# DeltaNet output gated by z where it is turned, q and k norms on VectorE, and no two-tensor work on GpSimd in the attention of a hybrid encoder step

## The chip, the core and the metric

The kernel runs on one core of one Trainium2 chip. The metric is the device time of one execution in microseconds (us). The core's engines have queues of their own, each worked off in order: TensorE (PE) multiplies and transposes, VectorE (DVE), ScalarE (ACT) and GpSimd (POOL) work on elements, and SyncE (SP) issues most of the DMAs. An instruction waits at the head of its queue until the semaphores that it names have been raised.

## What is computed

One layer of an encoder for 592 tokens of width 1024 (16 meta tokens and 512 of a prompt, and 64 of a sample stream with 256 cached keys). All of it is in float32.

```python
h = _rmsnorm(x, p["norm1"])
qa, ka, va, qkv_b, z_b, beta_b, alpha_b, gate_a, gate_b = jnp.split(h @ p["w_in"], SPLITS, axis=-1)
# branch A: differential attention, 8 heads, two 64-wide maps each
qa = _rmsnorm(qa.reshape(bsz, t, A_HEADS, 2, A_HEAD_DIM), p["q_norm"])
ka = _rmsnorm(ka.reshape(bsz, t, A_HEADS, 2, A_HEAD_DIM), p["k_norm"])     # also an output
o_a = attend(qa, ka, va, lam)
o_a = (_rmsnorm(o_a, p["sub_norm"]) * (1.0 - lam_init)).reshape(bsz, t, A_V_WIDTH)
# branch B: gated DeltaNet, 8 heads of 128
o_b, s_new = _gated_delta(qb, kb, vb, g, beta, ssm0.astype(f32))
z = jax.nn.silu(z_b.astype(f32)).reshape(bsz, t, B_HEADS, B_HEAD_DIM)
o_b = (_rmsnorm(o_b, p["gdn_norm"]) * z).reshape(bsz, t, B_WIDTH).astype(x.dtype)
# merge and channel mixer
mix = jax.nn.sigmoid(gate_a + p["b_gate"][0]) * (o_a @ p["w_br_a"]) + jax.nn.sigmoid(gate_b + p["b_gate"][1]) * (o_b @ p["w_br_b"])
x = x + mix @ p["w_out"]
h2 = _rmsnorm(x, p["norm2"])
x = x + jnp.square(jax.nn.relu(h2 @ p["w_up"])) @ p["w_down"]
```

## The kernel before

**Products in two parts.** Every large product is made of three: an operand x is kept as a high part in a reduced float32 format and the low part x minus high (names ending in h and l), and high x high, low x high and high x low are summed in PSUM. Weights come from DRAM in pieces of 128x1024 (wr), ScalarE casts the high part (wh), and the low part (wl) is subtracted by VectorE or GpSimd. `VG(out, n)` chooses between these two by the planned clocks of the engines.

**The stream of tasks and the chains.** `tasks` lists the large products in order: DeltaNet's q, k, v (pg_d), the gate z (pg_z), the attention's q, k, v for pairs of heads p (pg_a, the task names a, p and 0, 1 or 2), the merge gates B between them and A after them (pg_g), branch B (pg_bb), branch A (pg_ba), out (pg_o), up and down (pg_u, pa_dn to pd_dn). Beside them run chains, Python generators: the DeltaNet of four heads (`delta(0)`, `delta(1)`), for each head of the attention its preparation (`attend_prep`), 40 units of scores (`unit`, five for each head), the end of a head (`finish`), and `load_ob`. A planner (`Pace`) keeps a clock for each engine with fixed costs for instructions and transfers. `drive` writes some matmuls of the stream, then lets each chain whose last results are due by the planned clock of TensorE write its next stage. The order on every engine's queue comes out of this, before the kernel runs; it is not changed on the chip.

**Around the change.** `z_tasks` make z times (1 + tanh) of it, halved elsewhere, and store it in z_d. At the end of `delta(g)` the output of a tile of tokens (vtok) is scaled by its norm (c1), TensorE turns it (pf), ScalarE scales it by gdn_norm into oT, and SP stores it in ob_d. `load_ob` loads ob_d and z_d (tiles ma and mb), GpSimd multiplies them, and when the last task of gate A has read the hidden state (hh, hl), their high and low parts are written over it, for branch B. `attn_tasks` evict the projections (st) by a copy on ScalarE and store them in at_d; their squares give the norms' factors (rn). `attend_prep` loads q, k and v of a head, GpSimd multiplies q and k by rn and k by its weight (kn_bc), and k goes out as a result. Then TensorE turns k and q (ptk, ptq) and they are split (akT, aqT). A unit makes the scores (psc); VectorE adds the bias and takes the extremum (the ISA rows, `soft`), ScalarE exponentiates; VectorE joins the two maps (`combine`: mx<-mx,lam, then sc<-sc,mx); TensorE turns the weights (pwT), they are copied (wT), and it multiplies by v (ppo). `finish` makes a head's norm (aorv, aort, aory), scales (osb), turns (pot) and stores it in oa_d. The first three tasks of branch B may run beside the attention; the attention over, `load_oa` brings oa_d through two buffers (oa) and splits it (oh, ol) for branch A. Branch B's gate comes through tiles thb, its result goes to mb_d.

Of the kernel before, what the change touches and what calls it, by code (L numbers as in the profile page):

```python
# [17 lines left out]
P = 128  # L18
# [192 lines left out]
def stream_step_kernel(  # L211
# [74 lines left out]

    def VG(out, n):

        if "tail" in done:
            return V  # L290
        return V if max(pace.t["DVE"], pace.t["PE"]) + 1.05 * n <= max(pace.t["POOL"], pace.t["PE"]) + out * n else G

# [293 lines left out]
    th_d = [[dp.tile([P, TQ], F32, name=f"th_d{i}{j}") for j in range(KC)] for i in range(2)]  # L586
    qkv_d = [[dp.tile([P, 640 if i == 2 else T], F32, name=f"qkv_d{i}{j}") for j in range(4)] for i in range(3)]
    at_d = [dp.tile([H, P, NT, P], F32, name=f"at_d{i}") for i in range(3)]
    z_d, oa_d, mb_d = ([dp.tile([P, TQ], F32, name=f"{nm}{j}") for j in range(KC)] for nm in ("z_d", "oa_d", "mb_d"))
    ob_d = dp.tile([H, P, T], F32, name="ob_d")  # L590
    m_d = [dp.tile([4, 20, 32, 32], F32, name=f"m_d{i}") for i in range(2)]
    yi_d = [dp.tile([80, 1024], F32, name=f"yi_d{i}") for i in range(2)]
# [288 lines left out]
    def delta(g):  # L881
# [250 lines left out]
        r = rsqrt(db, c2, 20, 1.0 / P, EPS, tag="or")  # L1132
        V.scalar_tensor_tensor(c1, c1, 0.5, r, ALU.mult, ALU.mult)
        yield
        for s in range(NT + 1):
            if s:
                c0, n = TILES[s - 1]
                pf = bank(f"pf{g}{s}").rearrange("p (h i) -> p h i", h=4)
                for h in range(4):
                    TE.transpose(pf[:, h, :n], vtok[s - 1][:n, h], ident[:n, :n])  # L1140
                oT = a2(f"oT{s}")
                S.activation(oT[:, :, :n], pf[:, :, :n], AF.Copy, scale=gdn_col)
                store(ob_d[h0:h0 + 4, :, c0:c0 + n].rearrange("h d i -> d h i"), oT[:, :, :n])
            if s < NT:
                n = TILES[s][1]
                V.tensor_tensor(vtok[s][:n], vtok[s][:n], c1[:n, 4 * s:4 * s + 4, None].to_broadcast([n, 4, P]), ALU.mult)
            yield
# [31 lines left out]
    def z_tasks(cs):  # L1179
        out = []  # L1180
        for c in cs:
            def evac(h, ps, a, b, c=c):
                j = 2 * c + h
                if a == 0:
                    finish_convs(0)
                    gts["z"] = gp.tile([P, TQ], F32, name=f"zt{j}", tag="gth")
                th = gts["z"]
                S.activation(th[:, a:b], ps, AF.Tanh, scale=0.5)
                V.scalar_tensor_tensor(th[:, a:b], th[:, a:b], 1.0, ps, ALU.add, ALU.mult)
                if b == TQ:  # L1190
                    store(z_d[j], th)
                    done.add(f"z{c}")
            out.append(Task(f"z{c}", w_in[0], OFF_Z + c * 256, feat(hq, lq, f"z{c}", evac)))
        return out

# [3 lines left out]
    def attn_tasks(p):  # L1199
        def evac(i):  # L1200
            def f(t, n, ps):
                x = ep.tile([P, 256], F32, name=f"st{p}{i}{t}", tag="st")
                S.copy(x[:n], ps)
                xv = x.rearrange("t (h d) -> t h d", h=2)
                store(at_d[i][2 * p:2 * p + 2, :n, t].rearrange("h t d -> t h d"), xv[:n])
                if i < 2:
                    jk = ep.tile([P, 256], F32, name=f"sq{p}{i}{t}", tag="sq")
                    S.activation(jk[:n], ps, AF.Square)
                    V.tensor_reduce(rn[:n, p, i, t], jk[:n].rearrange("t (m d) -> t m d", d=64), AX.X, ALU.add)
                else:  # L1210
                    rows_out(p, t, n, xv, v_prompt, v_sample)
                if t == NT - 1:
                    if i == 1:
                        r = rn[:, p].rearrange("t i a m -> t (i a m)")
                        rsqrt(ep, r, 40, 1.0 / 64, EPS, tag="ar", out=r)
                    done.add(f"{'qkv'[i]}{p}")
            return f
        return [Task(f"a{p}{i}", w_in[0], off + p * 256, tok(hh, hl, f"a{p}{i}", evac(i)))
                for i, off in enumerate((OFF_QA, OFF_KA, OFF_VA))]
# [13 lines left out]
    def attend_prep(hd):  # L1233
# [12 lines left out]
        yield  # L1246
        for i in (1, 0):
            xv = x[i].rearrange("p t (m d) -> p t m d", d=64)
            G.tensor_tensor(xv, xv, rn[:, p, i, :, 2 * h:2 * h + 2, None].to_broadcast([P, NT, 2, 64]), ALU.mult)
        kv = k.rearrange("p t (m d) -> p (t m) d", d=64)  # L1250
        G.tensor_tensor(kv, kv, kn_bc[:, None, :].to_broadcast([P, 10, 64]), ALU.mult)
        store(k_prompt[0, 0, 0:80, hd], k[0:80, 0])
        store(k_prompt[0, 0, 80:464, hd].rearrange("(t r) d -> r t d", r=P), k[:, 1:4])
        store(k_prompt[0, 0, 464:528, hd], k[0:64, 4])
# [162 lines left out]

    def load_ob():

        while not has("delta0", "delta1", *[f"z{c}" for c in range(4)])():  # L1420
            yield
        obs = []
        for j in range(KC):
            obs.append(ab_.tile([P, TQ], F32, name=f"ma{j}", tag="ob"))
            b = ab_.tile([P, TQ], F32, name=f"mb{j}", tag="oz")
            Q.dma_start(obs[j], ob_d[j][:, N0:T])
            Q.dma_start(b, z_d[j])
            yield
            G.tensor_tensor(obs[j], obs[j], b, ALU.mult)
            yield  # L1430
        while "hidden" not in done:
            yield
# [246 lines left out]
        chains.append(Chain(conv_out()))  # L1679
        drive(lambda: not chains and has("delta0", "delta1")())  # L1680
    with pool("attn", side="right") as at_:
        ab_ = Tags(pace, at_, qk=4, v=3, past=3, sc=SC, mx=6, wT=WT, ob=8, oz=2, aoss=3, bias=2, osb=3,
                   aqT0=2, aqT1=2, akT0=2, akT1=2)
        done.add("attn")
        chains += [Chain(attend_prep(hd)) for hd in range(H)] + attend() + [Chain(load_ob())]
# [80 lines left out]
```

## Time and profile before

| | us |
|---|---|
| median of three runs (lowest to highest) | 1338.98 (1337.43 to 1342.21) |
| the profiled execution, device time | 1335.53 |
| its span, first to last instruction | 1333.6 |
| TensorE busy | 1286.3 (96%) |
| VectorE busy | 855.6 (64%) |
| ScalarE busy | 611.3 (46%) |
| GpSimd busy | 181.4 (14%) |
| mean granted TensorE clock | 0.986 of full speed |

Busy time is the time in which an engine worked on instructions. TensorE's clock is granted to it and can fall to half for a while; the stretches show it. The profile is one execution, and its microseconds are counted from its first instruction.

### The profile page before, as it was taken

The page shows a single profiled execution, that of the slowest core. Times are in us where ns is not written, and L with a number is a line of the kernel's source. Part 1 is how long each engine was busy: PE and PEld are TensorE (multiplying, and loading weights), DVE is VectorE, ACT ScalarE, POOL GpSimd, SP SyncE. Part 2 cuts the span into 40 slices and gives each one's busy share as a digit, 9 for nine tenths or more (in the row PEclk, how much of TensorE's full clock was granted, in tenths as well). Part 3 has the DMA queues.
Part 4 walks back from the last instruction along what each step waited for, and adds up shares of the span by engine and source line. Part 5 has one row for each costly group of instructions (what it writes and reads, how often), then busy time and mean ns, then how long its engine had stood idle before and what let it go on. Part 6 is the DMA issues. An engine that isn't in the chain of part 4 may idle for free.

```text
span 1333.6 us, 25734 instructions
## 1 busy us (share of the span) xinstructions
PE 1286.3 (96%) x10177; PEld 1242.1 (93%) x10177; DVE 855.6 (64%) x1842; ACT 611.3 (46%) x1438; POOL 181.4 (14%) x251
## 2 busy tenths in 40 slices
PE   7999999999999999999798997999999999999998
PEld 5989999999999999998787886999999999999998
DVE  5766999334377525267777853345678678678687
ACT  5565544333752333366465742224453443453442
POOL 3111513100330000252422102310000000000000
PEclk9999999999999999999899898999999999999999
DMA  6324244423644423774444336542223322323322
GB/s 165 91 67 155 61 145 129 144 81 88 206 118 135 144 60 95 228 235 129 161 131 142 122 124 211 182 141 80 80 80 95 96 80 87 105 62 97 110 76 76
DMA packets 163806, 160.55 MB, mean 120 GB/s; under 512 B 23531, under 2 KB 143613, under 8 KB 163686
## 3 DMA queue, kind: packets, MB, share of 16 engines
q1 hardware_dynamic: 161574, 153.11, 37.7%
q0 software_dynamic: 2112, 5.80, 1.5%
q8 instruction: 80, 1.31, 0.4%
q14 instruction: 40, 0.33, 0.1%
HBM read 123.94 MB, written 37.88 MB: 121 GB/s over the span
## 4 chain that ended last, share of the span: by engine, by line
PE 83%; DVE 6%; DMA 4%; ACT 3%; issue 2%; SPq 0%; POOL 0%; DVEq 0%; ACTq 0%; POOLq 0%
PE pg_u L165 15%; PE pg_a L165 11%; PE pg_d L165 8%; PE pg_g L165 7%; PE pg_ba L165 4%; PE pg_z L165 4%; PE pg_o L165 4%; PE pd_dn L165 4%; PE pa_dn L165 4%; PE pc_dn L165 4%; PE pg_bb L165 3%; PE ppo L165 2%; PE pb_dn L165 2%; DMA bias_d<-bv_d 2%; PE po L165 1%
## 5 line engine op out<-in xcount | busy, mean ns | idle before, releaser
L165 PE MATMUL pg_u<-h2h,wh_u 128*128 128x288 f32 x512 | 151.5, 296 | 0.0
L165 PE MATMUL pg_u<-h2h,wl_u 128*128 128x288 f32 x512 | 151.3, 296 | 0.0
L165 PE MATMUL pg_u<-h2l,wh_u 128*128 128x288 f32 x512 | 151.3, 295 | 0.0
L165 PE MATMUL pg_a<-wh_a,hh 128*128 128x256 f32 (+1 forms) x480 | 136.3, 284 | 1.3 <-ACT sq L165 1.3
L165 PE MATMUL pg_a<-wh_a,hl 128*128 128x256 f32 (+1 forms) x480 | 136.3, 284 | 0.0
L165 PE MATMUL pg_a<-wl_a,hh 128*128 128x256 f32 (+1 forms) x480 | 135.4, 282 | 0.0
L165 PE MATMUL pg_d<-hh,wh_d 128*128 128x336 f32 (+1 forms) x384 | 115.8, 302 | 0.0
L165 PE MATMUL pg_d<-hl,wh_d 128*128 128x336 f32 (+1 forms) x384 | 115.6, 301 | 0.0
L165 PE MATMUL pg_d<-hh,wl_d 128*128 128x336 f32 (+1 forms) x384 | 115.5, 301 | 0.0
L165 PEld LDWEIGHTS pg_u<-h2h,wh_u 128*128 128x128 f32 x512 | 96.1, 188 | 0.1
L165 PEld LDWEIGHTS pg_u<-h2l,wh_u 128*128 128x128 f32 x512 | 96.1, 188 | 0.0
L165 PEld LDWEIGHTS pg_u<-h2h,wl_u 128*128 128x128 f32 x512 | 96.1, 188 | 0.0
L165 PEld LDWEIGHTS pg_a<-wh_a,hh 128*128 128x128 f32 (+1 forms) x480 | 86.5, 180 | 2.4 <-ACT sq L165 1.9
L165 PEld LDWEIGHTS pg_a<-wh_a,hl 128*128 128x128 f32 (+1 forms) x480 | 86.6, 180 | 0.7 <-issue 0.6
L165 PEld LDWEIGHTS pg_a<-wl_a,hh 128*128 128x128 f32 (+1 forms) x480 | 86.5, 180 | 0.4 <-issue 0.2
L165 PE MATMUL pg_g<-hh,wl_g 128*128 128x288 f32 x256 | 78.2, 305 | 0.0
L165 PE MATMUL pg_g<-hh,wh_g 128*128 128x288 f32 x256 | 77.8, 304 | 0.0
L165 PE MATMUL pg_g<-hl,wh_g 128*128 128x288 f32 x256 | 77.7, 303 | 0.0
L165 PEld LDWEIGHTS pg_d<-hh,wl_d 128*128 128x128 f32 x384 | 72.9, 190 | 0.7 <-issue 0.6
L165 PEld LDWEIGHTS pg_d<-hl,wh_d 128*128 128x128 f32 x384 | 72.6, 189 | 1.0 <-issue 0.6
L165 PEld LDWEIGHTS pg_d<-hh,wh_d 128*128 128x128 f32 x384 | 72.7, 189 | 0.2
L165 DVE SCALAR_TENSOR_TENSOR cv_d<-pre_d,vec,cv_d 128x595 f32<-128x595 f32 x72 | 61.6, 861 | 14.7 <-ACT cv_d L165 7.9
(401 smaller groups left out, 3839.0 us busy)
## 6 DMA issues: line engine op xcount, KB each, us to landing
wr_u<-in_w_up_dram SPq DMA_DIRECT2D x32, 512.0 KB, 4.3
wr_dn<-in_w_down_dram SPq DMA_DIRECT2D x32, 512.0 KB, 3.7
wr_d<-in_w_in_dram SPq DMA_DIRECT2D x24, 512.0 KB, 5.1
wr_a<-in_w_in_dram SPq DMA_DIRECT2D x24, 512.0 KB, 3.7
wr_g<-in_w_in_dram SPq DMA_DIRECT2D x16, 512.0 KB, 5.8
at_d<-st SPq DMA_DIRECT2D x48, 128.0 KB, 2.5
th_d<-gt SPq DMA_DIRECT2D x16, 288.0 KB, 2.3
wr_z<-in_w_in_dram SPq DMA_DIRECT2D x8, 512.0 KB
```

The costliest lines, as they stand in the source:

```text
L165: r = f(*a, **kw)
```

## The change

z is kept in two tensors of four heads. `delta` waits for its z, loads it tile by tile (zl) one tile ahead, and VectorE multiplies the turned output by gdn_norm and z in one instruction straight from PSUM; oT is gone, and the store takes the rows from zl, without the meta tokens. `load_ob` loads no z and multiplies nothing. k's weight is multiplied in at the eviction of its projection, on VectorE instead of the copy on ScalarE. The norms of q and k are multiplied on VectorE. From the start of the attention to the merge `VG` returns VectorE.

```diff
--- before.py
+++ after.py
@@ -286,7 +286,7 @@
 
     def VG(out, n):
 
-        if "tail" in done:
+        if "tail" in done or "attn" in done and "merge" not in done:
             return V
         return V if max(pace.t["DVE"], pace.t["PE"]) + 1.05 * n <= max(pace.t["POOL"], pace.t["PE"]) + out * n else G
 
@@ -586,7 +586,8 @@
     th_d = [[dp.tile([P, TQ], F32, name=f"th_d{i}{j}") for j in range(KC)] for i in range(2)]
     qkv_d = [[dp.tile([P, 640 if i == 2 else T], F32, name=f"qkv_d{i}{j}") for j in range(4)] for i in range(3)]
     at_d = [dp.tile([H, P, NT, P], F32, name=f"at_d{i}") for i in range(3)]
-    z_d, oa_d, mb_d = ([dp.tile([P, TQ], F32, name=f"{nm}{j}") for j in range(KC)] for nm in ("z_d", "oa_d", "mb_d"))
+    oa_d, mb_d = ([dp.tile([P, TQ], F32, name=f"{nm}{j}") for j in range(KC)] for nm in ("oa_d", "mb_d"))
+    z_d = [dp.tile([4, P, TQ], F32, name=f"z_d{g}") for g in range(2)]
     ob_d = dp.tile([H, P, T], F32, name="ob_d")
     m_d = [dp.tile([4, 20, 32, 32], F32, name=f"m_d{i}") for i in range(2)]
     yi_d = [dp.tile([80, 1024], F32, name=f"yi_d{i}") for i in range(2)]
@@ -1132,15 +1133,24 @@
         r = rsqrt(db, c2, 20, 1.0 / P, EPS, tag="or")
         V.scalar_tensor_tensor(c1, c1, 0.5, r, ALU.mult, ALU.mult)
         yield
+        while not has(*[f"z{h0 + j}" for j in range(4)])():
+            yield
+        zls = {}
         for s in range(NT + 1):
+            if s < NT:
+                c0, n = TILES[s]
+                m0 = max(N0 - c0, 0)
+                zls[s] = a2(f"zl{s}")
+                Q.dma_start(zls[s][:, :, m0:n], z_d[g][:, :, c0 + m0 - N0:c0 + n - N0].rearrange("h d i -> d h i"))
             if s:
                 c0, n = TILES[s - 1]
+                m0 = max(N0 - c0, 0)
                 pf = bank(f"pf{g}{s}").rearrange("p (h i) -> p h i", h=4)
                 for h in range(4):
                     TE.transpose(pf[:, h, :n], vtok[s - 1][:n, h], ident[:n, :n])
-                oT = a2(f"oT{s}")
-                S.activation(oT[:, :, :n], pf[:, :, :n], AF.Copy, scale=gdn_col)
-                store(ob_d[h0:h0 + 4, :, c0:c0 + n].rearrange("h d i -> d h i"), oT[:, :, :n])
+                oT = zls.pop(s - 1)
+                V.scalar_tensor_tensor(oT[:, :, m0:n], pf[:, :, m0:n], gdn_col, oT[:, :, m0:n], ALU.mult, ALU.mult)
+                store(ob_d[h0:h0 + 4, :, c0 + m0:c0 + n].rearrange("h d i -> d h i"), oT[:, :, m0:n])
             if s < NT:
                 n = TILES[s][1]
                 V.tensor_tensor(vtok[s][:n], vtok[s][:n], c1[:n, 4 * s:4 * s + 4, None].to_broadcast([n, 4, P]), ALU.mult)
@@ -1188,8 +1198,8 @@
                 S.activation(th[:, a:b], ps, AF.Tanh, scale=0.5)
                 V.scalar_tensor_tensor(th[:, a:b], th[:, a:b], 1.0, ps, ALU.add, ALU.mult)
                 if b == TQ:
-                    store(z_d[j], th)
-                    done.add(f"z{c}")
+                    store(z_d[j // 4][j % 4], th)
+                    done.add(f"z{j}")
             out.append(Task(f"z{c}", w_in[0], OFF_Z + c * 256, feat(hq, lq, f"z{c}", evac)))
         return out
 
@@ -1200,7 +1210,11 @@
         def evac(i):
             def f(t, n, ps):
                 x = ep.tile([P, 256], F32, name=f"st{p}{i}{t}", tag="st")
-                S.copy(x[:n], ps)
+                if i == 1:
+                    kx, kp = (y.rearrange("t (h d) -> t h d", d=64) for y in (x[:n], ps))
+                    V.tensor_tensor(kx, kp, kn_bc[:n, None, :].to_broadcast([n, 4, 64]), ALU.mult)
+                else:
+                    S.copy(x[:n], ps)
                 xv = x.rearrange("t (h d) -> t h d", h=2)
                 store(at_d[i][2 * p:2 * p + 2, :n, t].rearrange("h t d -> t h d"), xv[:n])
                 if i < 2:
@@ -1246,9 +1260,7 @@
         yield
         for i in (1, 0):
             xv = x[i].rearrange("p t (m d) -> p t m d", d=64)
-            G.tensor_tensor(xv, xv, rn[:, p, i, :, 2 * h:2 * h + 2, None].to_broadcast([P, NT, 2, 64]), ALU.mult)
-        kv = k.rearrange("p t (m d) -> p (t m) d", d=64)
-        G.tensor_tensor(kv, kv, kn_bc[:, None, :].to_broadcast([P, 10, 64]), ALU.mult)
+            V.tensor_tensor(xv, xv, rn[:, p, i, :, 2 * h:2 * h + 2, None].to_broadcast([P, NT, 2, 64]), ALU.mult)
         store(k_prompt[0, 0, 0:80, hd], k[0:80, 0])
         store(k_prompt[0, 0, 80:464, hd].rearrange("(t r) d -> r t d", r=P), k[:, 1:4])
         store(k_prompt[0, 0, 464:528, hd], k[0:64, 4])
@@ -1417,16 +1429,12 @@
 
     def load_ob():
 
-        while not has("delta0", "delta1", *[f"z{c}" for c in range(4)])():
+        while not has("delta0", "delta1")():
             yield
         obs = []
         for j in range(KC):
             obs.append(ab_.tile([P, TQ], F32, name=f"ma{j}", tag="ob"))
-            b = ab_.tile([P, TQ], F32, name=f"mb{j}", tag="oz")
             Q.dma_start(obs[j], ob_d[j][:, N0:T])
-            Q.dma_start(b, z_d[j])
-            yield
-            G.tensor_tensor(obs[j], obs[j], b, ALU.mult)
             yield
         while "hidden" not in done:
             yield
@@ -1679,7 +1687,7 @@
         chains.append(Chain(conv_out()))
         drive(lambda: not chains and has("delta0", "delta1")())
     with pool("attn", side="right") as at_:
-        ab_ = Tags(pace, at_, qk=4, v=3, past=3, sc=SC, mx=6, wT=WT, ob=8, oz=2, aoss=3, bias=2, osb=3,
+        ab_ = Tags(pace, at_, qk=4, v=3, past=3, sc=SC, mx=6, wT=WT, ob=8, aoss=3, bias=2, osb=3,
                    aqT0=2, aqT1=2, akT0=2, akT1=2)
         done.add("attn")
         chains += [Chain(attend_prep(hd)) for hd in range(H)] + attend() + [Chain(load_ob())]
```

What this does to the queues is shown at three places; numbers behind an underscore only tell buffers apart, and the digit before it is the head or the piece.

The first is on GpSimd, where the fourth head (3) is prepared while the third head's (2) units run. Before:

```order
L165 MEMSET sc23_7888 128x64
L165 TENSOR_TENSOR ma5_7838<-ma5_7838,mb5_7839 128x576
L165 TENSOR_TENSOR k3_7810<-k3_7810,rn_94 128x640
L165 TENSOR_TENSOR q3_7809<-q3_7809,rn_94 128x640
L165 TENSOR_TENSOR k3_7810<-k3_7810,kn_bc_83 128x640
L165 TENSOR_TENSOR ma6_7951<-ma6_7951,mb6_7952 128x576
```

and with the change:

```order
L165 MEMSET sc22_7816 128x64
L165 MEMSET k3_7844 64x128
L165 MEMSET q3_7843 64x128
L165 MEMSET v3_7845 64x128
L165 MEMSET sc23_7918 128x64
L165 MEMSET oss3_8012 128x5
```

The two-tensor rows are gone, and memsets are left. On VectorE, at the end of the same units, the second head's norm (aorv, aory) stands before the join of unit 23 and its scores (sc23). Before:

```order
L165 ISA sc24_7907,mx24_7908<-psc2410_7900,bias2_7333 64x320
L165 ISA mx24_7908 64x1
L165 TENSOR_SCALAR aorv39_7914<-oss1_7051 128x5
L165 TENSOR_SCALAR aory41_7916<-aorv39_7914 128x5
...
L165 TENSOR_SCALAR aory41_7916<-aory41_7916 128x5
L165 RECIPROCAL mx23_7890<-mx23_7890 128x2
L165 SCALAR_TENSOR_TENSOR mx23_7890<-mx23_7890,lam_87 128x1
L165 SCALAR_TENSOR_TENSOR sc23_7888<-sc23_7888,mx23_7890 128x528
```

and with the change (in both the left-out rows are the rest of the norm, in the second the other scan rows too):

```order
L165 TENSOR_TENSOR k3_7844<-k3_7844,rn_94 128x640
L165 TENSOR_TENSOR q3_7843<-q3_7843,rn_94 128x640
L165 TENSOR_SCALAR aorv39_7956<-oss1_7102 128x5
L165 TENSOR_SCALAR aory41_7958<-aorv39_7956 128x5
...
L165 TENSOR_SCALAR aory41_7958<-aory41_7958 128x5
L165 ISA sc24_7985,mx24_7986<-psc2400_7977,bias2_7421 64x320
...
L165 TENSOR_TENSOR akT31_8010<-ptk30_8014,akT30_8009 128x464
L165 TENSOR_TENSOR akT31_8010<-ptk31_8021,akT30_8009 128x384
L165 RECIPROCAL mx23_7920<-mx23_7920 128x2
L165 SCALAR_TENSOR_TENSOR mx23_7920<-mx23_7920,lam_87 128x1
L165 SCALAR_TENSOR_TENSOR sc23_7918<-sc23_7918,mx23_7920 128x528
```

The norms of k and q came ahead of the second head's norm, and the low half of the fourth head's k (akT31) ahead of the join. The third place is SP's queue at the end of branch B, from the fourth load of the attention's output (oa3) on. Before:

```order
L165 DMA oa3_10149<-oa_d3_140 128x576
L165 DMA mb_d6_151<-thb6_10102 128x576
L165 DMA thb7_10168<-th_d17_113 128x576
L165 DMA oa4_10190<-oa_d4_141 128x576
L165 DMA mb_d7_152<-thb7_10168 128x576
L165 DMA oa5_10212<-oa_d5_142 128x576
L165 DMA oa6_10216<-oa_d6_143 128x576
L165 DMA oa7_10220<-oa_d7_144 128x576
```

and with the change:

```order
L165 DMA oa3_10158<-oa_d3_132 128x576
L165 DMA mb_d7_144<-thb7_10136 128x576
L165 DMA oa4_10180<-oa_d4_133 128x576
L165 DMA oa5_10184<-oa_d5_134 128x576
L165 DMA oa6_10188<-oa_d6_135 128x576
L165 DMA oa7_10198<-oa_d7_136 128x576
```

Behind the last store of branch B (mb_d7) stood three loads of oa, and now four. On TensorE's queue 168 matmuls of branch B stood behind the last turning of the attention's output (pot), and now 112 stand there; the count of all its rows, 8657, is the same. On VectorE the pair of norms stands eight times, the first two ahead of the first scores and six behind.

## Rows read from the trace of the kernel before

**Rows 1.** The page, busy us of engines (share of the span) and instructions.

```profile
PE 1286.3 (96%) x10177; PEld 1242.1 (93%) x10177; DVE 855.6 (64%) x1842; ACT 611.3 (46%) x1438; POOL 181.4 (14%) x251
```

**Rows 2.** Stretches: us, busy (instructions) by engine; then granted clock, DMA share, GB/s.

```profile
605.00:785.00 180.00, 161.55 (x1218) 142.88 (x1217) 139.64 (x460) 110.86 (x336) 42.90 (x69) 0.95 0.42 132
...
645.00:650.00 5.00, 5.00 (x30) 4.91 (x28) 3.32 (x9) 1.68 (x4) 0.00 (x0) 0.64 0.43 113
685.00:690.00 5.00, 4.78 (x28) 4.30 (x26) 2.21 (x11) 4.05 (x14) 0.00 (x0) 0.66 0.25 88
```

**Rows 3.** TensorE's waits, 560 to 790: total us, times, longest.

```profile
PE pwT L165 <- DVE sc L165: 6.6, 4, 5.0
PE pwT L165 <- DVE mx L165: 4.4, 2, 3.0
PE pg_bb L165 <- ACT hh L165: 2.9, 1, 2.9
PE psc L165 <- DVE mx L165: 1.7, 1, 1.7
...
PE pwT L165 <- DVE akT L165: 0.8, 1, 0.8
```

**Rows 4.** VectorE in order of time, 603 to 774: start, us, instruction.

```profile
603.50 1.16 DVE L165 SCALAR_TENSOR_TENSOR mx<-mx,lam 128x1 f32<-128x1 f32 x1
...
635.97 1.38 DVE L165 TENSOR_SCALAR aory<-aorv 128x5 int32<-128x5 int32 x1
637.38 1.18 DVE L165 SCALAR_TENSOR_TENSOR aort<-aory,aorv 128x5 f32<-128x5 f32 x1
638.60 1.19 DVE L165 TENSOR_TENSOR aort<-aort,aory 128x5 f32<-128x5 f32 x1
639.82 1.46 DVE L165 SCALAR_TENSOR_TENSOR aort<-aort 128x5 f32<-128x5 f32 x1
641.31 1.32 DVE L165 SCALAR_TENSOR_TENSOR aory<-aort,aory 128x5 f32<-128x5 f32 x1
...
773.55 2.39 DVE L165 SCALAR_TENSOR_TENSOR mx<-mx,lam 128x1 f32<-128x1 f32 x1
```

**Rows 5.** GpSimd in order of time, from 635 and at 773.

```profile
635.90 1.42 POOL L165 TENSOR_TENSOR ma<-ma,mb 128x576 f32<-128x576 f32 x1 [6.08 <-DMA mb<-z_d]
637.27 1.26 POOL L165 TENSOR_TENSOR k<-k,rn 128x640 f32<-128x640 f32 x1
...
639.72 1.53 POOL L165 TENSOR_TENSOR k<-k,kn_bc 128x640 f32<-128x640 f32 x1
...
773.55 2.38 POOL L165 TENSOR_TENSOR wl_bb<-wr_bb,wh_bb 128x1024 fp32r<-128x1024 f32 x1 [5.62 <-ACT wh_bb L165]
```

**Rows 6.** VectorE in order of time, at 776, GpSimd idle.

```profile
776.86 0.17 DVE L165 TENSOR_SCALAR aory<-aorv 128x5 int32<-128x5 int32 x1
```

**Rows 7.** Groups by shape on VectorE (before 600, from 550): busy, mean ns | idle before.

```profile
L165 DVE SCALAR_TENSOR_TENSOR mx<-mx,lam 128x1 f32<-128x1 f32 x4 | 0.9, 220 | 0.1
L165 DVE TENSOR_TENSOR R<-vT,pr 128x512 f32<-128x512 f32 x8 | 5.5, 685 | 15.5 <-PE pr L165 15.5
...
L165 DVE TENSOR_TENSOR wl_g<-wr_g,wh_g 128x1024 fp32r<-128x1024 f32 x5 | 6.1, 1214 | 0.0
L165 DVE TENSOR_TENSOR hl<-ma,hh 128x576 fp32r<-128x576 f32 x8 | 5.4, 751 | 1.8 <-ACT hh L165 1.8
```

**Rows 8.** The chain that ended last, 784 to 805: start, us, what.

```profile
793.84 9.69 PE pg_bb L165 x71
```

**Rows 9.** TensorE's waits, 790 to 840: total us, times, longest.

```profile
PE pg_ba L165 <- ACT oh L165: 5.4, 2, 3.5
PE pg_ba L165 <- DVE ol L165: 2.3, 4, 1.6
```

**Rows 10.** SP's queue in order of time, 820 to 830.

```profile
822.40 5.71 SPq L165 DMA_DIRECT2D oa<-oa_d x3
```

**Rows 11.** Waits from 550 to 890: total us, times, longest.

```profile
POOL k L165 <- DMA k<-at_d: 12.9, 4, 6.2
```

## The prediction

> **What bounds the kernel now.** I read the page first, then the stretches, then TensorE's waits, then the engines' rows around the longest of them. TensorE is busy for 96% of the span [rows 1], so a change that leaves its matmuls alone can only touch the time in which it stands, or in which it is granted less than full clock. The attention, from 605 to 785 us, is where it stands most: busy 161.55 of 180.00 us at a mean granted clock of 0.95, with VectorE (DVE) busy 139.64 us, 78% [rows 2]. In TensorE's waits of that stretch the reader is to see that DVE ends most of them: 6.6 + 4.4 + 1.7 + 0.8 = 13.5 us [rows 3]. ScalarE's hh, 2.9 us, is another matter: the split of the DeltaNet output for branch B, which the change keeps.
>
> Why DVE is late stands in its own rows. An instruction on five elements takes 0.17 us when GpSimd (POOL) is idle [rows 6]; between 635.97 and 641.31 five such took 1.38, 1.18, 1.19, 1.46 and 1.32 us [rows 4], and their ends step with POOL's two-tensor rows, which follow one another through the same microseconds [rows 5]. At 603.50 and 773.55 the one-column mx took 1.16 and 2.39 us, at the second place beside a POOL row of 2.38 [rows 4, 5], against 0.22 us in its undisturbed group [rows 7]. From 603.50 to 773.55 there are 19 DVE rows that last longer than their form does alone and overlap a POOL two-tensor row; their excess adds up to 21.0 us. The excess of the rows that run just before TensorE's six DVE waits is 17.4 us (5.7 of it ahead of the wait of 5.0 us), so TensorE pays 13.5 / 17.4 = 0.78 us for each that DVE loses there.
>
> The Trainium skill, page "SBUF — State Buffer", section "Who interferes with whom", says that a DVE instruction with two SBUF inputs contends with a GpSimd one that reads SBUF, that the later one waits for the whole of the other, and that a GpSimd instruction that only writes SBUF leaves it alone. By that rule the memsets that stay on POOL in the attention would cost DVE nothing, which no row here isolates. The sum would be the same without this rule.
>
> **The change, term by term.** The sum is against the profiled execution, 1335.5 us (span 1333.6 and 1.9 around it), which lies 3.5 us under the median of the runs shown, 1339.0.
>
> *POOL's two-tensor work leaves the attention*: the norms of q and k with k's weight, the gating of ma by mb, and the low halves of weights. All 13.5 us of waits on DVE came right behind blocked rows, each no longer than the excess before it or nearly so. Bounds: 0 if TensorE would have waited at the same places anyway, 13.5 if all go. I take 13.5, since a row that is not blocked can't be late by being blocked, and book what the new work costs separately: **-13.5**.
>
> *Clock.* After the wait of 5.0 us TensorE was granted 0.64 in 645 to 650, after that of 0.8 us on akT [rows 3] 0.66 in 685 to 690, busy in both [rows 2]; those are mixtures of its two levels, 1.2 and 2.4 GHz. They cost (1 - 0.64) x 5 + (1 - 0.66) x 5 = 3.5 us. Bounds 0 and 3.5; without the standing I expect all of it back: **-3.5**.
>
> *New work on DVE in the same stretch.* The norms on DVE are 128x640 two-tensor rows from SBUF. Between 128x576 at 0.75 us and 128x1024 at 1.21 [rows 7] that is 0.82 us. The order has eight pairs of them, and six pairs stand behind the first scores: 6 x 2 x 0.82 = 9.8 us. Four low halves, which POOL made in this stretch (the last at 773.55 [rows 5]), come to DVE: 4 x 1.21 = 4.9 us. Together 14.7 us, against 21.0 of blocking that goes: DVE gets lighter by 6.3 us, not heavier. But what stands behind a pair in DVE's queue (the rsqrt of a finished head, the next combine, and through that TensorE's transposes) is 1.64 us later. Bounds: 0 if every pair falls into DVE's own idle time, 40 of 180 us, and 0.78 x 14.7 = 11.5 if TensorE pays as it paid for blocking. At the place of the worst wait the order lets one judge it: DVE's excess was 5.7 us and the wait 5.0, so 0.7 us of slack were left; now a pair of norms (1.64) and the low half of the next head's k stand ahead of the combine, and TensorE has, besides the same 32 gate matmuls, the turning of that head's k and q and one more unit's value product to do meanwhile. Nearly covered there; other places will be less lucky, so I take a value nearer to the cover, under half: **+5.0**.
>
> *The hand-over to branch A.* After the attention's last turned output (pot) TensorE had 168 matmuls of branch B left before; now it has 112, since the order puts more of them inside the attention. At 9.69 us for 71 [rows 8] the 56 are 7.6 us of cover for the eight oa loads, which share two buffers. TensorE already waited 5.4 + 2.3 us for oh and ol there [rows 9]. The SP queue holds three oa loads behind the last mb store, in one row of 5.71 us from 822.40 [rows 10]; now it holds four. If the loads start with pot, 7.6 us are lost; if they end with the last mb store, which comes earlier with branch B, none is, as four loads on two buffers take the same two rounds as three. The stores and loads of thb stand between the oa loads in both orders, so I go nearer to none: **+3.0** (0 to 7.6).
>
> *Costed at nothing.* k's weight at the eviction replaces a ScalarE copy by a DVE product of 256 elements from PSUM, under the 0.69 us of one of 512 [rows 7]; 20 of them, each beside a block of 24 projection matmuls, with three PSUM banks as cover. Without these, each would cost at most that. The ten zl products do ScalarE's ten oT scalings on DVE for 0.69 us each; their z loads move from the attention's start into the DeltaNet tails. They are issued one tile ahead; if they land late, the attention starts later (its first k loads reuse that memory), while projections and gates keep TensorE busy until 605 us. The price if that cover went is in the upper end.
>
> Sum: -13.5 - 3.5 + 5.0 + 3.0 = **-9.0 us**: 1326.5 on the profiled time, 1330 on the median of the runs.
>
> **Rivals.**
>
> *DVE becomes the bound and gives it all back.* TensorE pays 11.5 for the new rows, with the hand-over at 5.5: -17.0 + 11.5 + 5.5 = 0, 1339, or 1335 to 1343. For it: DVE is at 78% already, and the norms now sit ahead of rows that TensorE waits for. Against: its total falls by 6.3 us. The Trainium skill, page "Perfetto Trace Analysis", section "Optimizing Scalar/DVE Operations", advises moving work off a saturated DVE, and adds that between DVE and GpSimd this might not help as they share a port. By its first half this rival is the likelier, by its second mine; the blocked rows speak for the second.
>
> *Slower: DVE stands for the loads of k and q.* On POOL the k norms waited 12.9 us in four waits for the loads from at_d [rows 11], and nothing hung on that. On DVE a scan of a unit would hang behind it. By DVE's balance in place of the first three terms, 14.7 + w - 21.0, it turns at w = 6.3 us; with w = 12.9 it is +6.6, at 0.78 that is +5.1, and +3.0 at the hand-over makes +8: 1347. (With w = 0 the balance gives -6.3 x 0.78 = -4.9, with the clock and the hand-over -5.4: 1333.6, inside the forecast's own range.) Against: the planner writes the norms out only near the landing that it reckons, and POOL came early because it had little else to do.
>
> *Everything goes and nothing comes back*: -13.5 - 3.5 = -17.0: 1322. For it: DVE stands idle for 40 us of the stretch; against: its queue is in order, and a pair has no way to step aside.
>
> **How the numbers follow.** Forecast 0.60 (1324 to 1335, all faster), nothing back 0.08, DVE bound 0.18, loads on DVE 0.14. A measurement of this kernel tells about 0.3%, 4 us, from no change. Faster 0.60 + 0.08 = 0.68; same 0.18; slower 0.14. Time 1330; the range 1318 to 1343 leaves out the slow rival and little else, and the forecast's own is 1324 to 1335.
>
> **What would show it.** Right: in the attention no mx or aort row above 0.3 us, TensorE's waits on DVE's sc and mx under 6 us, the granted clock 1.00 from 640 to 690, DVE busy near 133 us in a stretch of the same work. Wrong: waits of k rows on DMA on DVE over 6 us; waits for oh and ol over 15 us; new waits of pwT for DVE of the old size with no blocked row before them, which would say that POOL was not what made TensorE wait.

## The result, and the profile after

The changed kernel took 1315.6 us (median of 4 runs, 1314.7 to 1321.4) beside 1338.2 for the kernel before in the same comparison: ratio 0.984, interval 0.982 to 0.986, 22.6 us faster. The forecast was 9 us faster and its range ended at 1318. The profiled execution took 1314.7 us for a span of 1312.9, 20.7 less than before. Times of runs are medians; one run of e4 below, 1544.5 us in a slow state with a mean granted clock of 0.75 where its others have 0.99, is left out.

The page's line of the changed kernel, as in [rows 1]:

```profile
PE 1277.6 (97%) x10177; PEld 1236.2 (94%) x10177; DVE 863.8 (66%) x1887; ACT 603.7 (46%) x1421; POOL 110.1 (8%) x207
```

TensorE has the same 10177 instructions and is busy 8.7 us less; its idle time fell by 12.0. GpSimd (POOL) gave up 71 us, VectorE (DVE) took up 8.

TensorE's waits in the changed kernel, from 560 to 840 us, which answer to [rows 3, 9]:

```profile
PE pg_ba L165 <- ACT oh L165: 6.7, 2, 4.9
PE pg_bb L165 <- ACT hh L165: 1.7, 1, 1.7
PE ptk L165 <- DVE mx L165: 1.6, 1, 1.6
PE ptk L165 <- issue: 1.2, 1, 1.2
PE pg_ba L165 <- DVE ol L165: 0.9, 4, 0.4
PE pg_bb L165 <- DVE hl L165: 0.4, 1, 0.4
PE ppo L165 <- DVE mx L165: 0.3, 1, 0.3
PE pwT L165 <- DVE mx L165: 0.2, 1, 0.2
```

The waits on DVE's sc and mx went from 12.7 us to 2.1. The wait for hh is 1.2 us shorter. The waits for oh and ol are 7.6 us after 7.7.

DVE in order of time where the norms of a head stand, ahead of the same rsqrt steps as in [rows 4]:

```profile
640.98 0.83 DVE L165 TENSOR_TENSOR k<-k,rn 128x640 f32<-128x640 f32 x1
641.72 0.82 DVE L165 TENSOR_TENSOR q<-q,rn 128x640 f32<-128x640 f32 x1
...
642.66 0.17 DVE L165 TENSOR_SCALAR aory<-aorv 128x5 int32<-128x5 int32 x1
```

The norms cost the 0.82 us that the prediction took from two other shapes, and the five-element rows are back at 0.17.

Stretches of the changed kernel, columns as in [rows 2], the engines in the order of the page's line: from the first gate matmul (pg_g) to the first of the output projection (pg_o); the attention from its first ptk to its last pot; then the two places where [rows 2] has 0.64 and 0.66; then the start of branch B and the wait at branch A.

```profile
415.24:865.60 450.36, 436.80 (x3622) 411.47 (x3621) 270.88 (x779) 215.67 (x572) 25.77 (x74) 0.98 0.51 158
574.39:782.04 207.65, 201.74 (x1598) 182.19 (x1597) 157.03 (x553) 135.43 (x406) 7.97 (x56) 0.99 0.50 159
...
645.00:650.00 5.00, 5.00 (x41) 5.00 (x42) 3.20 (x12) 4.37 (x15) 0.00 (x0) 1.00 0.24 64
685.00:690.00 5.00, 5.00 (x45) 4.22 (x44) 3.45 (x14) 3.62 (x11) 0.46 (x4) 1.00 0.46 133
...
710.00:715.00 5.00, 5.00 (x33) 4.91 (x32) 4.93 (x10) 3.96 (x9) 0.67 (x5) 0.77 0.19 70
805.00:810.00 5.00, 2.17 (x6) 1.50 (x6) 1.46 (x2) 1.92 (x4) 0.00 (x0) 0.50 0.43 137
```

The same stretches of the kernel before, and 735 to 745 us, where branch B starts there:

```profile
413.63:886.14 472.51, 444.00 (x3622) 416.92 (x3621) 270.57 (x752) 218.36 (x574) 91.72 (x115) 0.97 0.49 153
569.82:793.04 223.22, 204.64 (x1581) 183.94 (x1580) 167.92 (x544) 132.59 (x396) 61.12 (x93) 0.96 0.48 147
...
735.00:745.00 10.00, 7.00 (x31) 6.66 (x32) 8.13 (x14) 9.63 (x21) 3.65 (x4) 0.66 0.40 130
```

From pg_g to pg_o TensorE has the same work in all kernels below (3622 or 3623 recorded matmuls, in p3 3637), and there the changed kernel is 22.15 us shorter: 14.95 of idle time (28.51 to 13.56) and 7.20 of busy time. By the granted clock of windows of 2.5 us some 5.9 of the 7.20 is half clock. What runs ahead of pg_g took between 410.9 and 420.6 us in the profiled executions, in part from half clock that comes and goes with TensorE busy: from 260 to 280 us e1 and e3 were granted 0.74, before, f1 and the changed kernel 1.00, all busy for the whole 20 us. So the experiments are compared by the stretch from pg_g to pg_o ("the stretch" below) as well as by their medians. The stretch comes from one execution of each; where two kernels run the attention alike, its row repeats within 0.2 us (207.65, 207.85 and 207.76 in the changed kernel, h2 and h3).

### The profile page after: what moved, and what is told of

It reads as the page before. It is cut to its first block, busy times and chain, and to the rows that moved or that the text cites. A ratio compares the mean times of both kernels' runs of the same rounds, so it can differ in the third digit from the quotient of the medians.

```text
span 1312.9 us, 25759 instructions
## 1 busy us (share of the span) xinstructions
PE 1277.6 (97%) x10177; PEld 1236.2 (94%) x10177; DVE 863.8 (66%) x1887; ACT 603.7 (46%) x1421; POOL 110.1 (8%) x207
## 4 chain that ended last, share of the span: by engine, by line
PE 85%; DVE 6%; ACT 4%; DMA 3%; issue 1%; SPq 0%; POOL 0%; DVEq 0%; ACTq 0%; POOLq 0%
PE pg_u L165 16%; PE pg_a L165 11%; PE pg_d L165 9%; PE pg_g L165 7%; PE pg_ba L165 4%; PE pg_z L165 4%; PE pg_o L165 4%; PE pd_dn L165 4%; PE pa_dn L165 4%; PE pc_dn L165 4%; PE pg_bb L165 3%; PE ppo L165 2%; PE pb_dn L165 2%; ACT djk L165 2%; PE po L165 1%
## 5 line engine op out<-in xcount | busy, mean ns | idle before, releaser
L165 ACT CAST wh_dn<-wr_dn 128x1024 fp32r<-128x1024 f32 x32 | 33.6, 1050 | 81.4 <-DVE wr_dn L165 41.2
```

The lines of the kernel that those rows point to most:

```text
L165: r = f(*a, **kw)
```

## The experiments

The theory: GpSimd's two-tensor rows hold DVE up, TensorE waits for that and then runs at half clock; without them DVE has room for most of the new work. The rivals: the gain comes from the planner's other order; or from the z part, which moves loads and products out of the attention.

**GpSimd's rows made to write only, or not issued, in the kernel before.** The planner was still told of the old row, so that the order of every other engine is that of before.

```
-            G.tensor_tensor(xv, xv, rn..., ALU.mult)       # likewise kn_bc, mb and the low halves
+            only_write(xv, xv, rn...)      # e1: two memsets of the tile; f1: nothing (a memset for a low half)
```

> The kernel before with every engine's order of instructions kept; only what GpSimd runs in the attention changes: each of its two-tensor rows there (norms of q and k, k's weight, the gating of ma, the low halves that the planner gave it) is replaced by two memsets of the same tile, some 38 rows. So the norms, the gating and those low halves are left out. Contention (GpSimd's two-tensor rows hold VectorE up, and TensorE waits for that): TensorE's 13.5 us of waits on VectorE and the 3.5 to 5 us of half clock behind them go, about 1338 - 18 = 1320 us (1316 to 1325), and no one-column mx row above 0.3 us. Order (the gain of the change comes from the planner's other order, or from the moved z loads): nothing moves, 1338 within 4.

> The kernel before with every engine's order kept and GpSimd's two-tensor rows of the attention not issued at all (norms, k's weight and gating left out; the five low halves are replaced by one memset each). It gives the full size of the contention. If the memsets of the write-only kernel cost nothing: 1338 - 20 = 1318 us (1316 to 1320). If the small VectorE rows that stood beside them (2.8 us of excess) were paid for: 1315 to 1316. If the whole gain of the change, before what it pays for new work, is contention: 1315.6 - 4 = 1311.5 us.

Measured: e1 1317.3 us, ratio 0.985 (0.984 to 0.987); f1 1316.4 us, 0.984 (0.982 to 0.987). TensorE's waits in f1, from 400 to 850 us:

```profile
PE pg_ba L165 <- ACT oh L165: 5.3, 2, 3.3
PE pg_bb L165 <- ACT hh L165: 2.9, 1, 2.9
PE pg_ba L165 <- DVE ol L165: 2.3, 4, 1.6
PE pg_a L165 <- ACT sq L165: 1.1, 1, 1.1
PE pxr L165 <- DMA x_r<-in_x_prompt_dram: 0.8, 1, 0.8
PE pot L165 <- ACT wT L165: 0.7, 1, 0.7
PE pg_bb L165 <- DVE hl L165: 0.2, 1, 0.2
```

and its row from pg_g to pg_o:

```profile
415.61:867.38 451.77, 437.78 (x3622) 413.04 (x3621) 247.30 (x752) 217.67 (x574) 37.91 (x83) 0.98 0.52 160
```

No wait on sc, mx or akT is left, with before's order on every engine and the loads of z where they were. The stretch is 20.7 us shorter than before's: 14.5 of idle and 6.2 of busy time. Neither the planner's order nor the moved z part is needed for a gain of this size; that GpSimd made TensorE wait is shown, and its size is about 20 us, which both medians give too (20.1 and 19.8 us under before in the same comparison). e1's memsets cost nothing that the medians (0.9 us) or the stretch (451.94 us beside 451.77) tell. They write the same tiles at the same places in GpSimd's queue and keep it busy for 47.61 us of the attention, after 61.12 before, so it was not GpSimd's results that TensorE waited for, but what the two-tensor rows did to VectorE.

**The rows put back into the changed kernel, on a tile that nobody reads.**

```
+        beside(640, 640, 640, 576, y=v...)   # e2: nc.gpsimd.tensor_tensor(scr, scr, v...)
#                                             # e3: a copy of one element of v, then memsets of scr
```

> The changed kernel with all its orders kept, plus 37 two-tensor rows on GpSimd over a scratch tile that nobody reads, at about the places where the kernel before had them (per head three of 640 elements and one of 576, and five of 1024; nearly 60 us of GpSimd). Contention: the gain goes again for the most part, 1315.6 + 15 = 1331 us (1325 to 1337), with one-column rows of VectorE above 1 us. Order or the moved loads: 1315.6 within 3.

> The same as the kernel with the 37 scratch rows, but each two-tensor row is replaced by memsets of the scratch tile of about the same length together (and a copy of one element that keeps the place in time). If it is the reading of two tensors that holds VectorE up: 1315.6 within 3 us and no long one-column row. If any work of GpSimd on SBUF does: 1331 us, as with the two-tensor rows.

For each head these are four rows, and five more of 1024 elements stand beside low halves (shortened here). Measured: e2 1359.5 us, ratio 1.016 (1.015 to 1.018), 44 us over the changed kernel where 15 were expected; e3 1319.2 us (1316.5 to 1326.6), 0.987 (0.985 to 0.989). In e2, GpSimd and DVE in order of time:

```profile
647.71 7.36 POOL L287 TENSOR_TENSOR scr<-scr,v 128x640 f32<-128x640 f32 x4 [0.94 <-DMA v<-at_d]
```

```profile
647.91 1.38 DVE L165 SCALAR_TENSOR_TENSOR mx<-mx,lam 128x1 f32<-128x1 f32 x1
649.33 2.00 DVE L165 SCALAR_TENSOR_TENSOR sc<-sc,mx 128x400 f32<-128x400 f32 x1
651.25 2.55 DVE L165 TENSOR_TENSOR wl_g<-wr_g,wh_g 128x1024 fp32r<-128x1024 f32 x1
```

These three DVE rows take 0.22, 0.63 and 1.22 us in the changed kernel. Counted over the attention, as rows that are over 0.15 us longer than their form is alone and overlap a two-tensor row of GpSimd, DVE's excess is 39.8 us in e2, 23.7 before (21.0 in the prediction's shorter stretch), none in the changed kernel and in f1. And GpSimd's rows grow as well: 7.36 us for four, where rows of these lengths took 1.26 to 1.58 us each before, for the most part. The attention's rows in e2 and e3 show where the time went:

```profile
572.59:826.45 253.86, 219.50 (x1597) 196.83 (x1596) 196.31 (x554) 137.55 (x406) 68.94 (x93) 0.89 0.41 130
579.73:793.71 213.98, 205.91 (x1598) 186.19 (x1597) 160.14 (x553) 135.65 (x406) 68.45 (x163) 0.97 0.49 155
```

In e2 idle time is 34.4 us, after 5.9 in the changed kernel, and the busy time grew by 17.8 at a granted clock of 0.89: to 28.5 us more of standing the clock added more than half as much again.

The direction is the theory's; the size was missed, since the expectation had priced the rows by what they cost before. About as many rows took 16 us more from DVE here than before. Up to 9.6 us of the 39.8 fell on DVE's new rows (norms 5.6, low halves at most 4.0), and 7.0 on a place: GpSimd's rows now ran beside the split of the DeltaNet output (hl), which they had not met before. In e2, then before:

```profile
737.29 12.42 DVE L165 TENSOR_TENSOR hl<-ma,hh 128x576 fp32r<-128x576 f32 x8 [0.23 <-ACT hh L165]
```

```profile
737.80 5.44 DVE L165 TENSOR_TENSOR hl<-ma,hh 128x576 fp32r<-128x576 f32 x8 [1.83 <-ACT hh L165]
```

So what such a row costs depends on what VectorE has to do while it runs.

The Trainium skill, page "SBUF — State Buffer", section "Who interferes with whom", has it that a DVE instruction with two SBUF inputs contends with a GpSimd one that reads SBUF, not with one that only writes. e2 against e3 agrees: 44 us against 3.6 by the medians. By the stretch it is 47.4 against 6.6 us, in e3's profiled run of 1326.6, 1.7 of it idle time and the rest half clock, so that writing costs much less is shown, and that it costs nothing is not.

**One part of the change at a time.** p1 has only the low halves on DVE (the one line of VG), p2 only the norms with k's weight at the eviction, p3 only the z part, p4 all but the z part.

> The kernel before with one part of the change: no low half of weights on GpSimd in the attention (five rows, 12 of the 56 us of GpSimd's two-tensor work there). Contention, shared out by GpSimd's busy time and with the 20 us that the write-only rows gave back: 20 x 12 / 56 = 4.3, less 0.34 us for each of four or five low halves on VectorE, so about 1337.5 - 3 = 1334.5 us (1331 to 1337). Order alone: 1337.5 within 4.

> The kernel before with one part of the change: the norms of q and k on VectorE and k's weight at the eviction (24 GpSimd rows go, 33 of 56 us). Contention: 20 x 33 / 56 = 11.8 back, and 1.5 to 4.5 paid for the new rows (what leaving them out of the changed kernel gave): 1337.5 - 9 = 1328.5 us (1325 to 1333). If the norms on VectorE are the ones that now collide with the GpSimd rows that stay (gating and low halves): no gain, 1333 to 1340.

> The kernel before with one part of the change: z gates the DeltaNet output where it is turned (eight GpSimd rows of the attention go, 11 of 56 us, with eight z loads there). Contention: 20 x 11 / 56 = 4 back: 1333.5 us (1330 to 1337). If the moved z products and their loads are worth more than the contention (the 5 us by which the parts that were priced so far fall short of the whole): 1325 to 1329.

> The changed kernel without its z part: z still gates in the attention, by GpSimd rows of 576 elements, the only two-tensor work of GpSimd left there. Contention, shared by busy time: 1315.6 + 4 = 1319.6 us (1317 to 1324), with long VectorE rows only beside those eight. If VectorE's new two-tensor rows make each of these eight worse, as the scratch rows showed (44 us for 37 rows, 1.2 us a row): 1315.6 + 8 x 1.2 = 1325 us.

Measured, beside 1338.2 of before: p1 1327.1 (ratio 0.991, 0.989 to 0.994), p2 1323.9 (0.989, 0.986 to 0.992), p3 1331.4 (0.994, 0.992 to 0.997), p4 1321.3 (0.987, 0.985 to 0.990). The parts alone give 11.1 + 14.3 + 6.8 = 32.2, the whole 22.6: the gains do not add up. DVE's excess is 16.7, 17.2, 16.6 and 2.8 us in p1 to p4. p3 and p4 came within what was expected. Sharing the gain out by GpSimd's busy time failed for p1 (3 us expected, 11 measured) and p2 (9 and 14); the planner's order differs in each of these, and whether the place of the rows or that order made the rest is open. The z part is worth 5.7 us on top of the other two, where its share of the excess is 2.8; whether the rest is the moved loads or the order is not shown.

**Less and more of the new work on DVE.** In e4 the norms are left out of the changed kernel, in d1 the norms and the five low halves that GpSimd had made (a memset on GpSimd stands for each of the five); in d2 each norm runs twice. The planner was told the same in all three, so all other rows keep their order.

```
-            V.tensor_tensor(xv, xv, rn..., ALU.mult)                 # e4, d1
+            nc.vector.tensor_tensor(scr, xv, rn..., ALU.mult)        # d2, beside it
```

> The changed kernel with the 16 norm rows of q and k on VectorE left out (so q and k are not normalised), every other row in the same order on every engine. It prices the term that the prediction booked at +5.0: if TensorE pays for this work as booked, 1315.6 - 5 = 1310.6 us; if VectorE does it in its idle time, 1315.6 within 1.5.

> The changed kernel with nearly all of VectorE's new work in the attention left out: the 16 norm rows and the five low halves that GpSimd made before (the norms and those halves are left out; five memsets on GpSimd stand in their place, all other rows keep their order). If the low halves cost TensorE as the norms did (4.5 us for 16 rows of 0.82): 1315.6 - 4.5 - 2 = 1309 us. If the norms alone are what counts: 1311 within 1.5, as without the norms. If the 4.5 us were mostly scatter: 1313 to 1315.

> The changed kernel with each of the 16 norm rows issued a second time on VectorE, into a scratch tile that nobody reads, all else in its order: 13 us more of VectorE in the attention. If work there is paid for at the rate that leaving it out gave (0.28 to 0.34 us of TensorE for each us of VectorE): 1315.6 + 4 = 1319.6 us. If VectorE has room: 1315.6 within 2. If it is at its limit, so that a further row is paid for as a blocked one was (0.8 to 1): 1326 to 1329.

Measured: e4 1310.7 us, d1 1311.9 (ratio 0.979, 0.977 to 0.982), d2 1322.9 (0.988, 0.986 to 0.990). The longest of TensorE's waits in d1, from 560 to 840 us, and the rows from pg_g to pg_o and of the attention:

```profile
PE pg_ba L165 <- ACT oh L165: 4.4, 2, 2.6
PE pg_ba L165 <- DVE ol L165: 2.6, 4, 1.9
PE pg_bb L165 <- ACT hh L165: 1.7, 1, 1.7
```

```profile
412.34:858.41 446.07, 436.22 (x3622) 411.77 (x3621) 254.04 (x758) 215.67 (x572) 30.26 (x79) 0.98 0.52 159
571.49:774.27 202.78, 200.08 (x1598) 181.55 (x1597) 141.78 (x534) 135.38 (x406) 11.84 (x62) 0.99 0.51 161
```

The new work costs 450.36 - 446.07 = 4.3 us by the stretch, 3.7 by the medians (the intervals of d1 and the changed kernel only just part). It is not free, as the changed kernel's list of waits alone might suggest. How it divides between norms and low halves stays open: e4's median puts all of it on the norms, its stretch (448.92) a third. The second set of norms costs 7.3 us by the medians, 9.7 by the stretch: the first 15.3 us of DVE work (157.03 against 141.78 busy in the attention) cost 0.28 us for each us, the next 12.1 cost 0.6 to 0.8, near the 0.78 that the prediction reckoned for a blocked one. DVE's room is nearly used up.

**The hand-over to branch A.** h2 has eight oa buffers and all eight loads up front; h3 has the loads on GpSimd's DMA queue; f2 holds branch B's third block of columns back as its fourth is, so that more of it covers the loads; f3 is h2 and f2 together.

```
-            Q.dma_start(a, oa_d[j])                # two buffers, one load per turn
+            for j in range(KC): Q.dma_start(oas[j], oa_d[j])     # h2, oa=8
+            G.dma_start(a, oa_d[j])                              # h3
-HELD = 3
+HELD = 2                                                         # f2
```

> The changed kernel with eight buffers for the oa loads in place of two, all eight issued at once ahead of the last mb stores. It tells what the wait of 7.6 us at branch A hangs on. If on the two buffers' rounds of loading and turning, and on SP's order: the waits for oh and ol go but for a rest, with the half clock behind them (3.0): 1315.6 - 8 = 1307.6 us (1305 to 1311). If on the cover, as the prediction's term had it (branch B's matmuls left after the last turned output; 16.6 us of TensorE here): 1315.6 within 2.

> The changed kernel with the eight oa loads on GpSimd's DMA queue, two buffers as before, the order of all engines' work unchanged: no oa load stands behind an mb store in SP's queue. If SP's order is what makes branch A wait: 1315.6 - 5 = 1310.6 us. If it is the two buffers (a load of 4 us for each round): 1315.6 within 2, or some us slower where GpSimd's queue holds the loads up.

> The changed kernel with branch B's third column block held back until the attention's memory is given up, as its fourth is: 192 matmuls of branch B behind the attention's last turned output in place of 112, 80 x 0.136 = 10.9 us more of cover for the oa loads, the same two buffers. If cover counts as the prediction had it (us for us): TensorE's waits for oh and ol go from 7.6 us to none, with some of the half clock: 1315.6 - 8 = 1307.6 us. If the loads end with the last mb store whatever the cover: waits of 6 to 8 us, 1315.6 within 2. In both cases a wait inside the attention may grow, since TensorE has 80 matmuls less to fill it with.

> The changed kernel with both: 192 matmuls of branch B behind the last turned output, and eight buffers for the oa loads, issued at once. If the rest of 4.2 us that eight buffers left is cover: no wait for oh or ol, 1315.6 - 10 = 1305.6 us. If that rest hangs on VectorE's own queue: 1311 within 2.

Measured: h2 1311.1 us (ratio 0.979, 0.977 to 0.982), h3 1316.0 (0.983, 0.981 to 0.986), f2 1320.3 (0.988, 0.986 to 0.991), f3 1318.4 (0.986, 0.984 to 0.988). SP's queue in the changed kernel, then in f2, which answer to [rows 10]:

```profile
800.32 0.32 SPq L165 DMA_DIRECT2D mb_d<-thb  x1
800.74 7.53 SPq L165 DMA_DIRECT2D oa<-oa_d  x4
```

```profile
808.58 0.32 SPq L165 DMA_DIRECT2D mb_d<-thb  x1
808.99 0.88 SPq L165 DMA_DIRECT2D oa<-oa_d  x2
```

In each the last oa loads stand right behind the last mb store. TensorE's waits for oh and ol in f2:

```profile
PE pg_ba L165 <- ACT oh L165: 4.3, 3, 2.7
...
PE pg_ba L165 <- DVE ol L165: 2.0, 3, 1.6
```

With 80 matmuls, 10.9 us, more of cover these waits are 6.3 us after 7.6: here cover counts for about a tenth of itself. f2 came out above both of its expectations, since it loses elsewhere what it moved: pot waits 2.5 us for DVE's osb and ppo 2.3 for wT, which they do not in the changed kernel. In h2 the eight loads leave SP at 782.50 in one row, and the wait for oh is gone:

```profile
782.50 3.74 SPq L165 DMA_DIRECT2D oa<-oa_d  x8
```

```profile
PE pg_ba L165 <- DVE ol L165: 4.2, 2, 2.2
```

Its stretch is 446.38, 4.0 shorter, and its median 4.5 lower; half of the 8 us that were expected. h2 is the fastest version here that computes all of the reference, though the two intervals (0.977 to 0.982 and 0.982 to 0.986) only just part. In h3 the waits for oh and ol fell to 3.7 us, but 3.2 came back as a wait for x_r, which shares that queue. f3 missed both of its expectations too (1305.6 and 1311): its waits for ol fell to 2.7 us, but f2's waits at pot and ppo stay, and its stretch is 455.57 us, 1.1 under f2's.

## Why the prediction was wrong in size

| term of the sum | forecast, us | by the stretch, us | from |
|---|---|---|---|
| GpSimd's work leaves, with the clock | -13.5 - 3.5 = -17.0 | -20.7 | before to f1 |
| new work on DVE | +5.0 | +4.3 | d1 to the changed kernel |
| hand-over (+3.0), and what was booked at nothing | +3.0 | -5.7 | f1 to d1 |
| sum | -9.0 | -22.15 | |

By the medians the three terms are -19.8, +3.7 and -4.5 us, with before itself between 1336.2 and 1338.3 in these comparisons.

**What held.** The cause: blocked DVE rows made TensorE wait. Three of the signs that were named for it came: no mx or aort row above 0.3 us in the attention, 2.1 us of waits on sc and mx, granted clock 1.00 from 640 to 690 us. The fourth was passed: DVE was to get lighter by 6.3 us, and in the attention it got lighter by 10.9. So neither the rival in which DVE becomes the bound nor the one in which it stands for loads came up (none of its waits is for k or q). The price of the new rows, +5.0 out of 0 to 11.5, came within about a microsecond; its two bounds came from rows and the value between them from judgement, so that it came so near is in part luck.

**What failed first: the hand-over, "+3.0".** The step took branch B's matmuls after the last pot as cover, and priced part of the 56 that moved away. f2 shows that cover is hardly what decides: the oa loads go round on two buffers with mb stores between them and end behind the last one, whenever that comes. The prediction had this as its zero bound ("if they end with the last mb store") and then took a value above it. In idle time the hand-over did not lose 3 us but gained 1 (8.62 after the last pot before, 7.65 now).

**What failed with it: waits booked at nothing.** The wait for hh was set aside as "another matter", of a split "which the change keeps", and those for sq, x_r and wT were not in the sum. Between f1 and d1, which have no two-tensor row on GpSimd in the attention and none of the new work on DVE there, the idle time is 4.1 us apart (13.99 and 9.85): the wait for hh 2.9 and 1.7, sq at pg_a 1.1 and none, x_r 0.8 and none, wT 0.7 and none, oh and ol 7.6 and 7.0. Busy time adds 1.6, of which some 1.3 is half clock by windows of 2.5 us. That these waits shrank is shown. For hh the planner's order alone is enough: p1, which changes neither ScalarE's evictions nor the z part, has it at 1.4 us (p2 and p4 at 1.1 and 1.5, p3 at 2.9). What shrank the others, the order or ScalarE's 20 fewer evictions, is not settled.

**What was mis-sized: the contention, by 3.7 us.** The idle part was near (14.5 for 13.5), and so was the clock: by the granted clock of windows of 2.5 us, 3.3 to 3.6 us of half clock went between before and f1, for a term of 3.5. But the stretch's busy time fell by 6.2 when the same order ran without the blocked rows. The other 2.6 or so had no term in the sum; it lies in busy rows at a clock that reads as full, and stays unexplained.

## What to carry to other kernels

Price a wait together with the busy time behind it: here each 10 us of standing came with 4 to 6 us more of busy time, much of it at half clock. Where a planner sets the order, a wait elsewhere that an edit "keeps" can move as well, so a comparison needs a kernel that has the old order without the suspected cost; telling the planner of a row and not issuing it gives that. Before moving two-tensor work between GpSimd and VectorE, see that VectorE has room for it, and read which of its rows run beside what stays on GpSimd: the amount alone said little, as some 55 us of it cost 20 us in the kernel before and not much more of it cost 44 when put into the changed one. Parts of the move were worth having too: p1 and p2 alone gained 11 and 14 us.

## What the runs showed of the hardware

GpSimd's memsets are not always free for DVE. In e3 a five-element row with one SBUF input took 0.98 us, after 0.17 alone, while memsets ran from 720.68 to 724.93, and the one behind it 0.97; the two-input row ahead of them (0.64, alone 0.63) did not grow. DVE, then GpSimd, in order of time:

```profile
722.41 0.64 DVE L165 SCALAR_TENSOR_TENSOR sc<-sc,mx 128x400 f32<-128x400 f32 x1
722.96 0.98 DVE L165 TENSOR_SCALAR aorv<-oss 128x5 f32<-128x5 f32 x1
723.98 0.97 DVE L165 TENSOR_SCALAR aory<-aorv 128x5 int32<-128x5 int32 x1
```

```profile
720.68 4.25 POOL L290 MEMSET scr<- 128x576 f32 x5
```

In e1 and e3 together, 13 rows grew beside memsets, by 0.2 to 0.8 us: 12 of TENSOR_SCALAR, none with two inputs, and one reciprocal, which started while a TENSOR_SCALAR that grew still ran and ended with it. Their excess is 2.8 us in e1 and 3.3 in e3. The Trainium skill's section named above says that copies, casts and tensor_scalar can take the shared pair of ports too, in modes that use two, and then contend with GpSimd; the traces agree for tensor_scalar, at five elements too.
